# The S5 recurrence of a four-branch backbone: the blocked complex scan on VectorE and GpSimd becomes one scan instruction per row on turned inputs

## The chip, the cores and the metric

One core of a Trainium2 chip runs the whole program. The metric is the device time of one execution in microseconds. Three runs of the kernel before took 2464.4, 2462.11 and 3806.75 us, so the median is 2464.4 us.

The engines are named as in the profile: PE is TensorE (matmul) and PEld its weight load, DVE is VectorE, ACT is ScalarE, POOL is GpSimd, and SP is SyncE, whose queue issues nearly every DMA of this program.

## The reference, cut to what matters

There are two layers over 2048 latent tokens and 256 context tokens, with 1024 channels. Layer 0 is a Fourier mixer beside a neighbourhood attention. Layer 1 is a gated MLP (spatial gating within chunks of 128 tokens) beside a bidirectional S5, a bank of linear recurrences with complex states. The change is in S5 alone:

```python
def linear_scan(lam_bar, bu, h0, reverse):
    """h_t = lam_bar * h_{t-1} + bu_t along axis 1 (or reversed). bu: (B, L, G, P) complex; h0: (B, G, P) or None."""
...
def s5_direction(u_lat, u_ctx, ...):
    lam_bar, b_bar = s5_discretise(lam_re, lam_im, log_step, b_re, b_im)
...
    h_ctx = linear_scan(lam_bar, drive(u_ctx), None, reverse)
    h_end = h_ctx[:, 0] if reverse else h_ctx[:, -1]
    h_lat = linear_scan(lam_bar, drive(u_lat), h_end, reverse)
    return read(h_lat), (read(h_ctx) if with_ctx_out else None)
```

There are 32 groups of 16 channels, 64 complex states in each group and two directions. `drive` multiplies the inputs with B, `read` multiplies the states with C and keeps the real part. After it come GELU, a gated linear unit (GLU) and the output projection.

## The kernel before, in words

**Eight tokens at a time.** The kernel folds eight tokens into one step of the recurrence, so a sequence of 2304 tokens has 288 steps, and the factor between steps is the eighth power of a state's own factor. Three constant matrices per group are made once from the S5 weights by `s5_prep` and kept in DRAM: `min_d` (inputs of eight tokens to the drive of a step), `mo_d` (states to outputs) and `kp_d` (inputs to outputs inside a step). `s5_prep` runs early, at about 140 to 330 us, woven between the projections `v_proj(0)`, `v_proj(1)` and `v_proj(2)` of layer 0. Right after `v_proj(2)` comes `fourier_first`: 16 pieces, each with a load of a DFT table (`d`, L559), a load of `Z` (L561), two matmuls (L564), a copy to `a` (L566) and a write to `A_d` (L567), and then the context's part (L573, L577).

**The S5 stage.** `odd` calls `s5_quarter` four times (j = 0 to 3, eight groups each). In a quarter PE computes the drive (`pd`, L1634: 4 matmuls for each of 4 pairs of groups and 2 directions), ACT copies it to the tile `S` (L1636: 128 partitions x 2 directions x real/imaginary x 4 pairs x 288 steps), and then the recurrence runs in place on `S`, in three parts:

- The 288 steps are cut into 18 blocks of 16. Inside all blocks at once, 15 steps of complex multiply-add run over strided columns: per step five DVE instructions (L1655 to L1660), three of 128x288 and two of 128x144, whose columns lie 16 numbers apart.
- The blocks' last states are chained: 17 steps of five tiny DVE instructions on the same lines (128x16 and 128x8).
- The state before each block is multiplied into the block (L1697 to L1700), for direction 0 on DVE in instructions of 128x1020 and for direction 1 on POOL in instructions of 128x510.

The tables of the factor's powers are `pa`, from `pa_d` in DRAM. Then `O<-S` DMAs (L1710) bring real and imaginary parts of one group under each other, and for each of the quarter's 8 groups three matmuls make the output (`pg`, L1718 with `T`, L1719 and L1720 with `mo` and `O`), ACT applies GELU into `z` (L1722), DVE takes its maximum (L1723, `zmax`), and a DMA writes `z`.

**What runs beside it.** The eight `odd_pair` calls (256 tokens each) are the gated MLP: PE matmuls `pu` of 512 columns and, for the first four pairs, `pg` of 256 columns (`gd_pair`). Their DVE work is statistics (L1576), a chain of tiny instructions for a reciprocal root (`rs`, L122 to L136), and the gates (`Gs`, L1594 and L1598); two multiplications per 128 tokens are on POOL (L1588, L1607). Matmuls of a later pair wait for `Gs` of the pair before, because `Gs` frees their PSUM bank. After S5 come `glu`, which needs all of `z`, and `final`.

**What sets the order.** A scheduler places every instruction when the program is built, by its own estimate of time; at run time each engine and the SP queue work strictly in that order and wait at semaphores. An instruction that waits holds up everything behind it on its engine. Pools of SBUF that open after others have closed share their space, and a tile there waits until the old tiles under it are done with.

Of the kernel before, what the change touches and what calls it, by code (L numbers as in the profile page):

```python
# [9 lines left out]
F32 = mybir.dt.float32  # L10
# [4 lines left out]
OP = mybir.AluOpType  # L15
# [39 lines left out]
class Kern:  # L55
# [1060 lines left out]
    def s5_prep(self, between):  # L1116
# [7 lines left out]
        self.pa_d = self.dram.tile([128, 4, 2 * 2 * 2 * 4 * 17], F32, name="pa_d")  # L1124
        with self.pool_("s5p") as pool, ExitStack() as early:
# [46 lines left out]
            L8 = t([128, 2, 16, 32])  # L1172
            nc.vector.tensor_copy(L8[:, :, 0], PW[:, :, 8])
            for w in (1, 2, 4, 8):
                double(L8, 0, w)

            pa = t([128, 4, 2, 2, 2, 4, 17])
            L8r = t([128, 2, 16, 16])
            for i in range(16):
                nc.gpsimd.tensor_copy(L8r[:, :, i], L8[:, :, 15 - i, 16:32])  # L1180
            for part in range(2):
                for d in range(2):
                    src = L8[:, part, :, d * 16:(d + 1) * 16]
                    for rd in range(2):
                        nc.vector.tensor_copy(pa[:, :, part, d, rd, :, 16], src[:, 0].rearrange("p (j g) -> p j g", j=4))
                        v = src if d == 0 else L8r[:, part]
                        nc.vector.tensor_copy(pa[:, :, part, d, rd, :, 0:16], v.rearrange("p i (j g) -> p j g i", j=4))
            self.bq.dma_start(self.pa_d, pa.rearrange("p j a d r g i -> p j (a d r g i)"))
# [95 lines left out]
        with self.pool_("s5pk") as pool:  # L1284
# [11 lines left out]
            for q in range(8):  # L1296
# [18 lines left out]
                self.bq.dma_start(self.kp_d[q], kp)  # L1315

# [160 lines left out]
    def odd(self, mw):  # L1477
# [139 lines left out]
    def s5_quarter(self, pool, pb, j):  # L1617
        nc = self.nc
        pa = pool.tile([128, 2, 2, 2, 4, 17], F32, name=self.name("pa"), tag="pa", bufs=2)
        nc.sync.dma_start(pa, self.pa_d[:, j].rearrange("p (a d r g i) -> p a d r g i", a=2, d=2, r=2, g=4))  # L1620

        S = pb.tile([128, 2, 2, 4, 288], F32, name=self.name("S"), tag="S", bufs=2)
        for gp in range(4):
# [5 lines left out]
            for d in range(2):  # L1629
# [6 lines left out]
                nc.scalar.activation(S[:, d, :, gp, :], ps[:, :, 0:288], AF.Copy)  # L1636
        DS, RS = 8 * 288, 4 * 288
        t1 = pool.tile([128, 4 * 17 * 15], F32, name=self.name("t1"), tag="t1", bufs=1)
        t2 = pool.tile([128, 4 * 17 * 15], F32, name=self.name("t2"), tag="t2", bufs=1)

        def ap(off, dstep, n, step):
            return bass.AP(tensor=S.tensor, offset=S.offset + off, ap=[list(S.ap[0]), [dstep, 2], [288, 8], [step, n]])

        def half(off, dstep, n, step):
            return bass.AP(tensor=S.tensor, offset=S.offset + off, ap=[list(S.ap[0]), [dstep, 2], [288, 4], [step, n]])

        def tab(part):
            return pa[:, part]

        def step(cur, prev, ar, ai, n):  # L1650

            m = 16 * n
            x1 = t1[:, 0:m].rearrange("p (d q n) -> p d q n", d=2, q=8)
            x2 = t2[:, 0:m].rearrange("p (d q n) -> p d q n", d=2, q=8)
            nc.vector.tensor_tensor(x1, ap(*prev), ar, op=OP.mult)  # L1655
            nc.vector.tensor_tensor(x2, ap(*prev), ai, op=OP.mult)  # L1656
            nc.vector.tensor_tensor(ap(*cur), ap(*cur), x1, op=OP.add)  # L1657
            nc.vector.tensor_tensor(half(*cur), half(*cur), x2[:, :, 4:8], op=OP.subtract)  # L1658
            c2 = (cur[0] + RS,) + cur[1:]
            nc.vector.tensor_tensor(half(*c2), half(*c2), x2[:, :, 0:4], op=OP.add)  # L1660

        ar = [tab(p)[:, :, :, :, 16].rearrange("p d r g -> p d (r g)")[:, :, :, None].to_broadcast([128, 2, 8, 18])
              for p in range(2)]
        for i in range(1, 16):
            step((i, DS + 15 - 2 * i, 18, 16), (i - 1, DS + 17 - 2 * i, 18, 16), ar[0], ar[1], 18)
        a16 = [tab(p).rearrange("p d r g i -> p d (r g) i") for p in range(2)]

        def last(p):

            x = a16[p]  # L1670
            return bass.AP(tensor=x.tensor, offset=x.offset + 15, ap=[list(x.ap[0]), [8 * 17 - 15, 2], [17, 8], [1, 1]])

        ll = [last(0), last(1)]
        for k in range(1, 18):
            step((16 * k + 15, DS + (17 - k) * 16 - (16 * k + 15), 1, 1),
                 (16 * k - 1, DS + (18 - k) * 16 - (16 * k - 1), 1, 1), ll[0], ll[1], 1)
        for d in range(2):

            cur0 = d * DS + (16 if d == 0 else 1)
            car0 = d * DS + (15 if d == 0 else 16)  # L1680

            def v(off, q, i):
                return bass.AP(tensor=S.tensor, offset=S.offset + off,
                               ap=[list(S.ap[0]), [288, q], [16, 17], [1, 15] if i else [0, 15]])

            i0 = 0 if d == 0 else 1
# [184 lines left out]
```

## Time and profile before

| What | Value |
|---|---|
| median of the three runs | 2464.4 us |
| the profiled execution, its own time | 2459.69 us |
| its span, first to last instruction | 2457.9 us |
| PE busy | 2223.6 us (90%), 15860 matmuls |
| DVE busy | 1625.8 us (66%), 4343 instructions |
| POOL busy | 445.7 us (18%), 533 instructions |
| mean granted TensorE clock | 0.96 of full speed |

Busy time of PE includes matmuls that run at the lower clock, and their ends are modelled; so a stretch in which PE is busy throughout can still be one in which it does less than it could. What PE could do is read from the distance between the starts of consecutive matmuls where nothing holds it up. A row of the list by stretches gives busy time and count of each engine, the granted clock, the share of the DMA engines and GB/s.

### The profile page before, as it was taken

The page shows a single profiled execution, that of the slowest core. Times are in us where ns is not written, and L with a number is a line of the kernel's source. Part 1 is how long each engine was busy: PE and PEld are TensorE (multiplying, and loading weights), DVE is VectorE, ACT ScalarE, POOL GpSimd, SP SyncE. Part 2 cuts the span into 40 slices and gives each one's busy share as a digit, 9 for nine tenths or more (in the row PEclk, how much of TensorE's full clock was granted, in tenths as well). Part 3 has the DMA queues.
Part 4 walks back from the last instruction along what each step waited for, and adds up shares of the span by engine and source line. Part 5 has one row for each costly group of instructions (what it writes and reads, how often), then busy time and mean ns, then how long its engine had stood idle before and what let it go on. Part 6 is the DMA issues. An engine that isn't in the chain of part 4 may idle for free.

```text
span 2457.9 us, 43136 instructions
## 1 busy us (share of the span) xinstructions
PE 2223.6 (90%) x15860; PEld 1421.2 (58%) x15860; DVE 1625.8 (66%) x4343; ACT 1047.0 (43%) x2208; POOL 445.7 (18%) x533
## 2 busy tenths in 40 slices
PE   5999997998999999999878999978968787999998
PEld 2667784675766666666564566666534443544443
DVE  5888413466576666766686767751799998457555
ACT  4822232455556565555565555532211211244232
POOL 0123100122222222222340000000053154110000
PEclk8999998999999999999988999989989888999999
DMA  9845756224343343523433435552234532556332
GB/s 321 255 119 147 192 166 177 69 74 135 83 139 99 93 140 102 138 76 102 155 113 102 164 124 138 163 175 91 79 87 124 143 98 79 147 151 206 116 116 90
DMA packets 344165, 324.98 MB, mean 132 GB/s; under 512 B 93154, under 2 KB 290158, under 8 KB 343058
## 3 DMA queue, kind: packets, MB, share of 16 engines
q1 hardware_dynamic: 343842, 322.20, 44.1%
q8 instruction: 125, 2.05, 0.3%
q14 instruction: 86, 0.70, 0.1%
q10 hardware_dynamic: 112, 0.03, 0.0%
HBM read 210.10 MB, written 102.59 MB: 127 GB/s over the span
## 4 chain that ended last, share of the span: by engine, by line
PE 60%; DVE 22%; DMA 8%; issue 3%; ACT 3%; SPq 2%; POOL 1%; DVEq 0%; ACTq 0%; POOLq 0%
PE pg L181 36%; PE pu L181 6%; PE S L997 4%; PE PT L1016 4%; DVE S L1657 2%; PE pv L1030 2%; DVE t L1655 2%; DVE t L1656 2%; DVE S L1658 2%; DVE wl L190 1%; PE pa L331 1%; DMA wf<-in_w_in_even_dram 1%; DVE S L1660 1%; PE pv L1033 1%; DMA s_d<-s 1%
## 5 line engine op out<-in xcount | busy, mean ns | idle before, releaser
L181 PEld LDWEIGHTS <-wh 128*128 128x128 f16 x2944 | 280.0, 98 | 168.3 <-issue 10.8
L1000 DVE CUSTOM_DVE_ANT_0 P<-S,bias,slab 128x640 f32<-128x640 f32 (+2 forms) x216 | 193.6, 896 | 162.6 <-PE S L997 161.5
L189 ACT ACTIVATE ph<-PT 128x384 f16<-128x384 f32 (+1 forms) x408 | 172.6, 457 | 217.2 <-PE PT L1016 216.2
L181 PE MATMUL pu<-wh,h1p 128*128 128x512 f16 x768 | 191.2, 397 | 45.0 <-DVE Gs L1594 42.5
L181 PEld LDWEIGHTS <-h1p 128*128 128x128 f16 x1152 | 115.2, 101 | 192.4 <-issue 72.9
L949 POOL TENSOR_TENSOR bias<-G,masks 128x384 f32<-128x384 f32 (+1 forms) x144 | 152.6, 1060 | 349.6 <-DVE t L1000 326.9
L181 PEld LDWEIGHTS <-wl 128*128 128x128 f16 x1472 | 142.7, 100 | 116.2 <-issue 31.9
L190 DVE SCALAR_TENSOR_TENSOR pl<-PT,ph 128x384 f16<-128x384 f32 (+1 forms) x408 | 195.1, 508 | 13.9 <-ACT ph L189 12.5
L1002 ACT ACTIVATE P<-P,t 128x640 f32<-128x640 f32 (+2 forms) x216 | 181.2, 839 | 40.2 <-DVE t L1000 38.9
L181 PE MATMUL pg<-hh,wl 128*128 128x512 f16 (+1 forms) x800 | 183.6, 363 | 15.6 <-DVE stg L190 7.5
L181 PE MATMUL pg<-hl,wh 128*128 128x512 f16 (+1 forms) x800 | 181.9, 361 | 0.0
L181 PE MATMUL pg<-hh,wh 128*128 128x512 f16 (+1 forms) x800 | 180.6, 358 | 0.0
L181 PEld LDWEIGHTS <-yh 128*128 128x128 f16 x1088 | 106.5, 98 | 124.3 <-issue 0.8
L1016 PE MATMUL PT<-ident,P 128*128 128x128 f32 x1104 | 162.8, 277 | 11.5 <-DVE pl L190 9.6
L997 PEld LDWEIGHTS <-Q 128*128 128x128 f16 x1776 | 132.7, 99 | 62.7 <-issue 22.0
L997 PE MATMUL S<-K,Q 128*128 128x128 f16 (+1 forms) x1776 | 160.2, 234 | 1.8 <-DVE t L1000 1.7
L181 PE MATMUL pg<-wh,yl 128*128 128x512 f16 x544 | 133.1, 386 | 5.2 <-DVE yl L190 5.1
L1016 PEld LDWEIGHTS PT<-ident,P 128*128 128x128 f32 x1104 | 120.6, 142 | 20.7 <-issue 8.4
L1037 POOL TENSOR_TENSOR o<-o 128x64 f32<-128x64 f32 x216 | 73.3, 339 | 323.9 <-ACT o L1036 322.6
L181 PE MATMUL pg<-wh,yh 128*128 128x512 f16 x544 | 130.3, 379 | 0.0
L181 PE MATMUL pg<-wl,yh 128*128 128x512 f16 x544 | 130.2, 379 | 0.0
L156 DVE TENSOR_REDUCE t<-wf 128x1 f32<-128x1024 f32 x68 | 82.5, 1216 | 71.9 <-DMA wf<-in_w_in_odd_dram 25.4
(341 smaller groups left out, 4168.3 us busy)
## 6 DMA issues: line engine op xcount, KB each, us to landing
wada<-in_w_ada_dram SPq DMA_DIRECT2D x34, 512.0 KB
x<-in_x_dram SPq DMA_DIRECT2D x32, 512.0 KB
wf<-in_w_in_even_dram SPq DMA_DIRECT2D x28, 512.0 KB
V<-vs SPq DMA_DIRECT2D x192, 64.0 KB
K<-kd SPq DMA_DIRECT2D x96, 128.0 KB
wf<-in_w_in_odd_dram SPq DMA_DIRECT2D x20, 512.0 KB
Y<-ys SPq DMA_DIRECT2D x144, 64.0 KB
O<-S SPq DMA_DIRECT2D x64, 144.0 KB
```

Source lines behind the costliest of these rows:

```text
L156: nc.vector.tensor_reduce(m[:, i:i + 1], f, axis=AX.X, op=OP.max, apply_absolute_value=True)
L181: nc.tensor.matmul(ps, a(k), b(k), start=(n == 0), stop=(n == 3 * kb - 1))
L189: nc.scalar.activation(hi, src, AF.Copy, scale=scale)
L190: nc.vector.scalar_tensor_tensor(lo, src, scale, hi, op0=OP.mult, op1=OP.subtract)
L949: nc.gpsimd.tensor_tensor(q4(bv), gv, q4(masks[:, m0:m0 + 128 * nch]), op=OP.add)
L997: nc.tensor.matmul(S[:, at:at + m], u["q"], K[:, hl, off:off + m], start=(hl == 1), stop=(hl == 0))
L1000: nc.vector.tensor_tensor_reduce(P[:, 0:n], S[:, 0:n], u["B"][:, 0:n], u["negf"], 3.4e38, OP.add, OP.min, nm)
L1002: nc.scalar.activation(P[:, 0:n], P[:, 0:n], AF.Exp, bias=nm, scale=-1.0, accum_out=l)
L1016: self.nc.tensor.transpose(PT[:, c - a:c - a + 128], P[:, c:c + 128], self.ident)
L1030: nc.tensor.matmul(pv, ph[:, i * 128:(i + 1) * 128], vals[i][:, hd * 128:hd * 128 + 128], start=(i == 0), stop=False, skip_group_check=True)
L1037: nc.gpsimd.tensor_tensor(o["t"][:, hd * 64:(hd + 1) * 64], o2[:, 0:64], o2[:, 64:128], op=OP.add)
L1655: nc.vector.tensor_tensor(x1, ap(*prev), ar, op=OP.mult)
```

## The change

The factor of a step is split into its magnitude and its angle. The inputs of the recurrence are first turned back by the accumulated angle of their step, which leaves a recurrence with a real factor for real and imaginary part apart; after it the states are turned ahead by the same angles. The real recurrence is one DVE instruction per row of 288 steps (`tensor_tensor_scan`, L1674 of the changed kernel, in the order's rows a SCALAR_TENSOR_TENSOR that reads `mag`); for direction 1 it reads and writes the row backwards.

- `s5_quarter` is gone. `odd` goes through 8 halves (a half is 2 pairs of groups): `s5_states`, then `s5_out`. `S` is now one tile per direction and half, in 5 buffers.
- Per half and direction DVE has: `turned` over 288 steps (two multiplications of 128x1152, an addition and a subtraction of 128x576), 4 scans of 128x288, and `turned` over 256 steps (two of 128x1024, two of 128x512). POOL has no part in it.
- Per half and direction a DMA loads the angle table `E` (590 KB). `pa` is gone.
- `O` is fetched without the columns that aren't used: eight DMAs of 64 x 1 KB per pair of groups instead of four of 64 x 2 x 1152 B.
- `s5_prep` makes the angle tables: the powers of the turned unit by doubling, in tiles `turn` that live until `s5_prep` ends, and at its very end 8 tables of 128x2304 by a complex product, six DVE instructions of 128x1152 each, with a DMA of 1.2 MB to `rot_d` after each. The doublings and copies for `pa`, 16 of them on POOL, are gone.

```diff
@@ s5_prep, tables
-            L8 = t([128, 2, 16, 32])
...
-            for i in range(16):
-                nc.gpsimd.tensor_copy(L8r[:, :, i], L8[:, :, 15 - i, 16:32])
...
-            self.bq.dma_start(self.pa_d, pa.rearrange("p j a d r g i -> p j (a d r g i)"))
+            for w in (1, 2, 4, 8):
+                double(R, 1, w)
...
+            for T, n, o in ((R, 16, turn[0]), (RB, 18, turn[1])):
+                for r in range(2):
+                    nc.scalar.activation(o[:, r], T[:, r, 0:n].rearrange("p k q -> p q k"), AF.Copy)
@@ s5_prep, its end (pool s5pk)
+            tp = [t([128, 4, 18, 16]) for _ in range(2)]
+            for j in range(4):
+                for d in range(2):
+                    e = pool.tile([128, 2, 4, 288], F32, name=self.name("rot"), tag="rot", bufs=2)
...
+                    self.cmul(nc.vector, [e[:, r].rearrange("p g (b k) -> p g b k", k=16) for r in range(2)], x, y, tp)
+                    self.bq.dma_start(self.rot_d[j, d], e.rearrange("p r g n -> p (r g n)"))
@@ odd
-                for j in range(4):
-                    self.s5_quarter(self.s5a, s5b, j)
+                for i in range(8):
+                    self.s5_out(self.s5a, s5b, i // 2, i % 2, self.s5_states(self.s5a, s5b, i // 2, i % 2))
@@ s5_states (was the first part of s5_quarter)
+        S = [pb.tile([128, 2, 2, 288], F32, name=self.name("S"), tag="S", bufs=5) for _ in range(2)]
...
+            e = pb.tile([128, 2, 2, 288], F32, name=self.name("E"), tag="E", bufs=3)
+            nc.sync.dma_start(e, dap(self.rot_d, ...
...
         for d in range(2):
+            self.turned(pb, S[d], E[d], 0, 288, False)
             for ri in range(2):
+                for g in range(2):
+                    x = S[d][:, ri, g, :] if d == 0 else self.reversed(S[d][:, ri, g, :])
+                    q = 16 * d + 4 * j + 2 * h + g
+                    nc.vector.tensor_tensor_scan(x, self.mag8[:, q:q + 1].to_broadcast([128, 288]), x, 0.0, OP.mult, OP.add)
+            self.turned(pb, S[d], E[d], 31 - 30 * d, 256, True)
@@ turned (new)
+        nc.vector.tensor_tensor(t, swap, e[1], op=OP.mult)
+        nc.vector.tensor_tensor(x, x, e[0], op=OP.mult)
+        op = (OP.subtract, OP.add) if ahead else (OP.add, OP.subtract)
+        for r in range(2):
+            nc.vector.tensor_tensor(x[:, r], x[:, r], t[:, r], op=op[r])
@@ s5_out (was the last part of s5_quarter)
-            O = pb.tile([128, 2, 2, 288], F32, name=self.name("O"), tag="O", bufs=3)
+            O = pb.tile([128, 2, 2, 256], F32, name=self.name("O"), tag="O", bufs=3)
...
-                for ri in range(2):
-                    nc.sync.dma_start(O[64 * ri:64 * ri + 64, gpar], S[64 * gpar:64 * gpar + 64, :, ri, gp, :])
+                for d in range(2):
+                    for ri in range(2):
+                        nc.sync.dma_start(O[64 * ri:64 * ri + 64, gpar, d],
+                                          S[d][64 * gpar:64 * gpar + 64, ri, gp % 2, 31 - 30 * d:287 - 30 * d])
```

The order of DVE where one part of S5 meets the next, before (`rs` and `Gs` belong to an `odd_pair`, `S` and `t` to S5):

```order
L1700 TENSOR_TENSOR S_23782<-S_23782,t_5000_23852 128x4x17x15
L1697 TENSOR_TENSOR t_4999_23851<-S_23782,pa_23780 128x1020
L1577 BN_AGGR t_25756<-t_25810 128x2
L1698 TENSOR_TENSOR t_5000_23852<-S_23782,pa_23780 128x1020
L1699 TENSOR_TENSOR S_23782<-S_23782,t_4999_23851 128x4x17x15
L122 TENSOR_SCALAR rs_25814<-t_25756,slab_18826 128x2
L1594 SCALAR_TENSOR_TENSOR Gs_25878<-Gs_25878,pu_25853 128x512
L1700 TENSOR_TENSOR S_23782<-S_23782,t_5000_23852 128x4x17x15
L1655 TENSOR_TENSOR t_5058_24235<-S_24166,pa_24164 128x288
L124 TENSOR_SCALAR rs_25816<-rs_25814 128x2
L1656 TENSOR_TENSOR t_5059_24236<-S_24166,pa_24164 128x288
L126 TENSOR_SCALAR rs_25818<-rs_25816 128x2
```

The same place in the changed kernel (L1689 to L1693 are `turned`, L1674 is the scan, L1620 is `Gs`):

```order
L1693 TENSOR_TENSOR S_23645<-S_23645,t_23685 128x576 x2
L122 TENSOR_SCALAR rs_24782<-t_24724,slab_18932 128x2
L1674 SCALAR_TENSOR_TENSOR S_23645<-mag_1850,S_23645 128x288 x4
L124 TENSOR_SCALAR rs_24784<-rs_24782 128x2
L1689 TENSOR_TENSOR t_23694<-S_23645,E_23647 128x4x256
L1723 TENSOR_REDUCE zmax<-z_23596 128x1
L126 TENSOR_SCALAR rs_24786<-rs_24784 128x2
L1690 TENSOR_TENSOR S_23645<-S_23645,E_23647 128x4x256
L130 TENSOR_TENSOR rs_24788<-rs_24786 128x2
L1693 TENSOR_TENSOR S_23645<-S_23645,t_23694 128x2x256 x2
L132 TENSOR_TENSOR rs_24790<-rs_24788,rs_24782 128x2
L1620 SCALAR_TENSOR_TENSOR Gs_24846<-Gs_24846,pu_24821 128x512
```

The pair's chain still goes through between pieces of S5, one instruction at a time; the pieces are others. On PE the last output matmul of S5 now stands behind 433 `pu` matmuls counted from the first `pd`, where 908 stood before; the `odd_pair` work that was ahead of it comes after it.

The order of the SP queue at the end of `s5_prep`, before (`chan`, `dctx`, `d` and `Z` are loads of `fourier_first`, `vs` is what `v_proj` writes):

```order
L552 DMA chan<-in_k_chan_dram 128x256
L554 DMA dctx<-in_k_dctx_dram 128x1024
L545 DMA vs_128<-v_3436 128x256
L545 DMA vs_129<-v_3436 128x256
L559 DMA d_639_4426<-in_k_dft_dram 128x256
L561 DMA Z_4428<-fa_d 128x256
L559 DMA d_643_4436<-in_k_dft_dram 128x256
L561 DMA Z_4438<-fa_d 128x256
L545 DMA vs_128<-v_3466 128x256
```

And in the changed kernel:

```order
L545 DMA vs_130<-v_4485 128x256
L545 DMA vs_131<-v_4485 128x256
L1340 DMA rot_d<-rot_3934 128x2304
L545 DMA vs_130<-v_4515 128x256
L545 DMA vs_131<-v_4515 128x256
L1340 DMA rot_d<-rot_3942 128x2304
L552 DMA chan<-in_k_chan_dram 128x256
L554 DMA dctx<-in_k_dctx_dram 128x1024
L559 DMA d_655_4532<-in_k_dft_dram 128x256
L561 DMA Z_4534<-fa_d 128x256
```

Before, the first loads of `fourier_first` stood among the writes of `v_proj(1)`, long ahead of the end of `v_proj(2)`; now they stand behind the last write of `v_proj(2)` (`v_4515`) and behind the last angle table. Accordingly all 32 matmuls of L564 stand in PE's order behind the last matmul of `v_proj(2)`, where before 15 of them stood between its groups.

## Rows read from the trace of the kernel before

**Rows 1.** The page, busy time by engine: us, share of the span, count.

```profile
PE 2223.6 (90%) x15860; PEld 1421.2 (58%) x15860; DVE 1625.8 (66%) x4343; ACT 1047.0 (43%) x2208; POOL 445.7 (18%) x533
```

**Rows 2.** Stretches: us, PE, PEld, DVE, ACT, POOL busy (count), PEclk, DMA share, GB/s.

```profile
1695.00:1735.00 40.00, 36.10 (x219) 20.06 (x220) 11.10 (x26) 10.69 (x14) 0.00 (x0) 0.90 0.36 121
1735.00:1800.00 65.00, 63.84 (x377) 33.55 (x376) 62.55 (x184) 14.12 (x26) 9.22 (x6) 1.00 0.25 79
2110.00:2185.00 75.00, 73.39 (x372) 39.22 (x371) 38.49 (x96) 23.51 (x39) 11.58 (x8) 1.00 0.51 137
```

**Rows 3.** One stretch, only instructions on S: us, PE, DVE, ACT, POOL busy.

```profile
1735.00:2110.00 375.00, 0.00 (x0) 282.16 (x672) 15.67 (x25) 107.74 (x64) 0.90 0.38 106
```

**Rows 4.** Waits of PE, 1735 to 2110 us: us in total, times, longest.

```profile
PE pu L181 <- DVE Gs L1594: 42.5, 7, 11.1
```

**Rows 5.** PE in order of time: start us, us, operation [idle before]. First drive, last output.

```profile
1696.31 2.19 PE L1634 MATMUL pd<-U,mi 128*64 128x288 f32 x8
...
2125.57 0.59 PE L1720 MATMUL pg<-O,mo 128*128 128x256 f32 x2
```

**Rows 6.** PE in order of time, rates: distances of starts at full clock.

```profile
1846.29 0.59 PE L1720 MATMUL pg<-O,mo 128*128 128x256 f32 x2
1846.72 0.60 PE L181 MATMUL pg<-h1p,wl 128*128 128x256 f16 x4
1847.15 0.82 PE L181 MATMUL pg<-h1p,wh 128*128 128x256 f16 x6
1847.90 1.19 PE L1634 MATMUL pd<-U,mi 128*64 128x288 f32 x8
1849.02 0.66 PE L1612 MATMUL pT<-ident,sy 128*128 128x128 f32 x4
...
2130.53 3.62 PE L181 MATMUL pu<-wh,h1p 128*128 128x512 f16 x16
2133.99 1.89 PE L181 MATMUL pu<-wl,h1p 128*128 128x512 f16 x8
```

**Rows 7.** DVE in order of time: plain and held-up instructions of the S5 stage.

```profile
1821.98 1.50 DVE L1656 TENSOR_TENSOR t<-S,pa 128x288 f32<-128x288 f32 x1
1823.40 1.08 DVE L136 TENSOR_TENSOR rs<-rs,rs 128x2 f32<-128x2 f32 x1
...
1825.00 0.63 DVE L1657 TENSOR_TENSOR S<-S,t 128x288 f32<-128x288 f32 x1
1825.55 0.15 DVE L130 TENSOR_TENSOR rs<-rs 128x2 f32<-128x2 f32 x1
```

**Rows 8.** DVE in order of time: contiguous operands of 512 columns.

```profile
150.62 0.69 DVE L1112 TENSOR_TENSOR p<-p,p 128x512 f32<-128x512 f32 x1
```

**Rows 9.** DVE groups by shape, 1340 to 1640 us: busy us, mean ns; 1024 columns.

```profile
L1339 DVE TENSOR_TENSOR x<-x,y 128x1024 f32<-128x1024 f32 x18 | 22.0, 1223 | 0.3
L156 DVE TENSOR_REDUCE t<-wf 128x1 f32<-128x1024 f32 x14 | 17.1, 1220 | 23.0 <-DMA wf<-in_w_in_odd_dram 22.9
```

**Rows 10.** POOL groups, 1735 to 2110 us: busy us, mean ns.

```profile
L1588 POOL TENSOR_TENSOR vc<-vc,sgg 128x512 f32<-128x512 f32 x12 | 16.6, 1403 | 494.9 <-ACT vc L1587 494.9
```

**Rows 11.** Stretches at the end of the preparation; columns as in rows 2.

```profile
282.00:328.00 46.00, 46.00 (x535) 40.56 (x533) 10.00 (x43) 15.81 (x43) 0.00 (x0) 1.00 0.70 180
328.00:361.00 33.00, 33.00 (x275) 29.09 (x273) 4.25 (x10) 8.06 (x18) 0.00 (x0) 1.00 0.49 153
361.00:377.00 16.00, 10.98 (x36) 8.07 (x35) 0.43 (x1) 5.40 (x10) 0.00 (x0) 0.79 0.67 221
```

**Rows 12.** PE in order of time: pieces of the Fourier step and what follows.

```profile
328.08 1.46 PE L564 MATMUL pg<-Z,d 128*128 128x256 f32 x6
...
360.76 2.32 PE L564 MATMUL pg<-Z,d 128*128 128x256 f32 x10
...
376.47 1.88 PE L573 MATMUL pg<-dctx,zc 128*128 128x512 f32 x4
```

**Rows 13.** One line's instructions: ns min/median/max, first and last start in us.

```profile
L1700 DVE TENSOR_TENSOR S<-S,t x8: 1208/1688/2085, 1802.4 to 2072.7; 128x1020 f32<-128x1020 f32 x8
```

More of the change, by code (lines that the diff above doesn't have):

```diff
@@ L1188, in s5_prep @@
-            self.bq.dma_start(self.pa_d, pa.rearrange("p j a d r g i -> p j (a d r g i)"))
+            sq = [t([128, 32]), t([128, 32])]
+            nc.vector.tensor_tensor(sq[0], mag, mag, op=OP.mult)
+            nc.vector.tensor_tensor(sq[1], sq[0], sq[0], op=OP.mult)
+            nc.vector.tensor_tensor(self.mag8, sq[1], sq[1], op=OP.mult)
+            R, RB = t([128, 2, 17, 32]), t([128, 2, 18, 32])
+            un = [t([128, 2, 32]) for _ in range(3)]
+            nc.vector.tensor_copy(un[0][:, 0], co)
@@ new lines, in s5_prep @@
+            nc.vector.tensor_copy(un[0][:, 1, 0:16], si[:, 0:16])
+            nc.vector.tensor_scalar(un[0][:, 1, 16:32], si[:, 16:32], -1.0, None, op0=OP.mult)
+            for k in range(3):
+                x = [un[k][:, r] for r in range(2)]
+                o = [un[k + 1][:, r] for r in range(2)] if k < 2 else [R[:, r, 1] for r in range(2)]
+                self.cmul(nc.vector, o, x, x, [z[:, 0] for z in tp])
+            for T in (R, RB):
+                nc.gpsimd.memset(T[:, 0, 0], 1.0)
+                nc.gpsimd.memset(T[:, 1, 0], 0.0)
@@ L1644, in half @@
[L1644 to L1671, printed above, removed]
@@ new lines, in reversed, with turned @@
+    def reversed(self, a):
+        n = a.shape[-1]
+        return bass.AP(tensor=a.tensor, offset=a.offset + n - 1, ap=[list(a.ap[0]), [-1, n]])
+    def turned(self, pb, S, E, at, n, ahead):
+        nc = self.nc
+        t = pb.tile([128, 2, 2, 288], F32, name=self.name("t"), tag="t", bufs=1)[:, :, :, 0:n]
+        x = S[:, :, :, at:at + n]
+        swap = bass.AP(tensor=x.tensor, offset=x.offset + 576, ap=[list(x.ap[0]), [-576, 2]] + [list(v) for v in x.ap[2:]])
+        e = [E[:, r, None, :, at:at + n].to_broadcast([128, 2, 2, n]) for r in range(2)]
+        nc.vector.tensor_tensor(t, swap, e[1], op=OP.mult)
[3 more added lines that the diff above has]
+            nc.vector.tensor_tensor(x[:, r], x[:, r], t[:, r], op=op[r])
@@ new lines, in s5_out @@
+    def s5_out(self, pool, pb, j, h, S):
+        nc = self.nc
+        if h == 0:
+            self.T = T = pool.tile([128, 8, 128], F32, name=self.name("T"), tag="T", bufs=1)
+            for s in range(8):
+                nc.sync.dma_start(T[16 * s:16 * s + 16], dap(self.kp_d, 8 * j * 32 * 240 + (7 - s) * 16,
+                                                            [[240, 16], [32 * 240, 8], [1, 128]]))
+        T = self.T
+        for gp in (2 * h, 2 * h + 1):
+            O = pb.tile([128, 2, 2, 256], F32, name=self.name("O"), tag="O", bufs=3)
```

78 lines of the change are left out of this document (25 added, 53 removed).

## The prediction

> **What bounds the kernel now.** By the page PE is the fullest engine and POOL the emptiest [rows 1], so the first question is whether the S5 stage is an exception. The list by stretches says that it is. From 1735 us on DVE is full, and at first PE is too, at the full clock [rows 2]. Then PE stops keeping up. Asked for the instructions on the tile S alone, the stretch 1735 to 2110 us shows 282.16 us of DVE and 107.74 us of POOL in 375 us, at a granted clock of 0.90 [rows 3]. PE's largest wait there is for `Gs`, 42.5 us in 7 pieces [rows 4]: `Gs` is the odd pairs' own work, which stands in DVE's queue between pieces of S5. POOL's part makes this worse: while it runs, a 128x2 instruction of the root chain takes 1.08 us and a 128x288 one 1.50 us, where 0.15 and 0.63 us are seen right after it has ended [rows 7].
>
> What PE loses is the distance between the work that it has and the time that it takes. At full clock a 512-column f16 matmul takes (2133.99 - 2130.53) / 16 = 0.216 us, a 256-column one 0.43 / 4 = 0.108, an f32 one of 256 columns 0.43 (each f32 matmul shows as two in a row's count), a drive matmul 1.12 / 4 = 0.28 [rows 6]. The program's order has, from the first drive to the last output of S5, 908 of the first kind (196 us), 384 (41), 96 (41) and 128 (36), and 96 small ones that I put at 0.16 us on the mean from L1612's row (15, so 329 in all). The trace shows 1696.31 to 2126.2, which is 430 us [rows 5]. So 101 us are lost. Of these some 8 belong to the start (PE is busy for 36.1 of the first 40 us, at 0.90 of the clock [rows 2]), which the change leaves alone. **At most about 91 us are to be had in this stage.**
>
> **The change, part by part.** The sum is made against the profiled execution, 2459.7 us; the median is 4.7 us above it.
>
> *DVE in the S5 stage.* Removed: what rows 3 show, 282 us on DVE and 108 on POOL. Added, per half and direction: two multiplications of 1152 columns, two of 576, two of 1024 and two of 512, all on contiguous operands. Plain contiguous instructions take 0.69 and 1.22 us for 512 and 1024 columns [rows 8, 9], that is 1.04 ns for a further column, so 0.76 us for 576 and 1.36 us for 1152. One half and direction takes 2 x (1.36 + 0.76 + 1.22 + 0.69) = 8.06 us, and 16 of them 129 us. Neighbours overlap by some 0.08 us, so I count 118. Then 64 scans of 288 columns, which no row shows. Low end: the contiguous rate, 0.69 - 224 x 1.04 ns = 0.46 us (29 us in all). High end: the slowest 288-column row, 1.50 us (96 us). I take the strided row of the same size, 0.63 us [rows 7], because a recurrence that needs its own last result is more likely below than at the full rate: 40 us. [...]
>
> Beside S5, DVE's order holds to the last piece about 36 us of the three or four odd pairs and of 27 maxima (50 instructions of 256 or 512 columns at 0.4 to 0.7 us, about 50 tiny ones at 0.15). POOL keeps two multiplications per 128 tokens at 1.40 us [rows 10]; in four pairs that is 16 x 1.4 = 22 us in which DVE runs at about half its rate, so 11 us more. DVE: 118 + 40 + 36 + 11 = 205 us, and it begins some 12 us after the first drive. PE's order holds to the last output 433 x 0.216 + 41 + 41 + 36 + 8 = 220 us. The two end together, at about 217 to 220 us. So PE becomes the bound, but narrowly, and each in-order queue still waits for the other at every half: S goes from PE by ACT to DVE, by the SP queue into `O`, and back to PE. I leave 15 us of the 91 as lost, between 0 (DVE always ahead) and 45 (half stays). The 110 us of `pu` matmuls that now come behind S5 run as the pairs at 2110 to 2185 us do, where PE is busy for 73.39 of 75 us [rows 2]: 3 us.
>
> *E, O and the SP queue.* 16 loads of 590 KB are new, 9.4 MB, and `O` takes 128 DMAs for 64. The DMA engines are at 0.38 in this stretch [rows 3]; the same traffic in 235 instead of 390 us gives 0.63, and E at the page's rates for such stages adds about 0.15. That fits. I cost it at nothing beyond the 15 us, since E is loaded a half ahead; if that cover is gone, the start of each half is late, and PE waits at L1719.
>
> *The preparation.* Powers by doubling for powers by doubling, POOL's 16 copies gone: near zero, and at best a gain of 4 us. New at its end: 8 x 6 multiplications of 1152 columns, 48 x 1.27 = 61 us of DVE, beside `v_proj(2)`. DVE is busy for 10 of 46 and 4.25 of 33 us there [rows 11], so it rises to about 75 of 79 us: it just fits. But `fourier_first` doesn't fit any more. Before, five groups of three L564 matmuls, 1.5 pieces each, ran between the projections at about 1.3 us a group (6.5 us of PE), and the other 8.5 pieces after 360.76 took 376.47 - 360.76 = 15.7 us, 1.85 each [rows 12], because loads and writes of three buffers pace them: PE is busy for 11 of 16 us and DMA at 0.67 [rows 11]. Now their loads stand on the SP queue behind the last angle table, and all 16 pieces come after the projections: 16 x 1.85 = 29.6 us in place of 15.7 + 6.5. That is 7.4 us more, plus about 3 us for the first load's landing and 2 us where 9.4 MB of table writes meet a DMA share of 0.70 [rows 11]. I take 12 us. Low end -4 (DVE ends early, loads keep ahead), high end +30 (the multiplications push the evictions of `v_proj(2)` as well).
>
> *Sum.* -91 + 15 + 3 + 12 = -61: 2398.7 us against the profiled execution, **2403 us** as a median.
>
> **The rivals.**
>
> 1. *The chain through DVE stays the bound.* If a scan takes 1.5 us, DVE's sum rises by 56 us to 261, some 50 us behind PE, and about half of the 91 us stays lost: 2440 to 2450 us. The same comes of an SP queue whose `O` fetches wait for S and hold up the loads behind them. For it: DVE and PE end within a few us of each other in my sum. Against: even then DVE has less than before. Chance 0.22.
> 2. *The preparation costs its high end.* 30 us in place of 12: about 2421 us. For it: DVE near full beside the evictions for 75 us, and a large write after each table. Chance 0.10.
> 3. *Slower than before.* A scan's step waits for the result of the step before it, and the latency isn't hidden. Before, S5's last DVE piece came 2072.7 - 1696.31 = 376 us after the first drive [rows 5, 13]; now DVE is at 12 + 165 us without scans, so the gain is used up, with 12 us of preparation, at 64 scans of 2.9 us, 10 ns for each step. At 5 us a scan DVE takes 320 us longer than without scans, and the time is about 2460 + 130 = 2590 us. For it: nothing in the trace is a true recurrence. Against: a reduction, which also carries a running value, takes 1.22 us for 1024 columns in rows 9, the rate of a plain addition. Chance 0.06.
> 4. *It doesn't free what it means to.* PE's wait at `Gs` is the pair's chain itself, 16 dependent instructions, and other waits move up: 2450 to 2465 us. Against: the chain is 16 x 0.15 us once POOL is quiet. Chance 0.04.
>
> **How the numbers follow.** The forecast has 0.58; its own range, from no stall and cheap preparation (2375) to the middle of both upper ends (2427), is met below 2415 in about nine of eleven cases. 2415 us is 2% below the median, and 2% is about what a measurement of this kernel can tell from no change. Faster by over 2%: 0.48 from the forecast, 0.04 from rival 2, 0.05 from rival 1 in its mild form, 0.57. Slower by over 2%: rival 3 and a little of unknown stalls, 0.07. Within 2%: 0.36. The range reaches from 2370 us to 2450 us, which takes in the upper end of rival 1 and leaves out rival 3, most of rival 4 and a gain beyond the 91 us.
>
> **What would show it.** Right: in the stretch of S5 the granted clock back near 1.00, PE's waits for `Gs` a few us in all, the last L1720 about 235 to 240 us after the first drive, scan rows (L1674) near 0.6 us, and L573 10 to 15 us later than 376 us. Wrong: DVE still at 95% and PE waiting at L1719 or for `Gs` (rival 1), waits of PE for `v` between 280 and 360 us (rival 2), scan rows of several us (rival 3). A forecast like this fails most easily where two engines come out within 5 us of each other on paper.

## The result, and the profile after

The changed kernel takes 2424.4 us (median of 4 runs, 2421.3 to 2431.3) where the kernel before took 2463.3 (median of 4), about 39 us less. By the fast runs alone, which leave out one of 3806.8 us of the kernel before, the ratio is 0.985, with a 95% interval of 0.982 to 0.988: faster, by less than 2%. The profiled execution took 2425.1 us with a span of 2423.3.

Three points on PE's own time line split the difference: L573, the first matmul behind the Fourier pieces, where the preparation ends; the first drive of S5; and the end of the span.

| | before | after | difference |
|---|---|---|---|
| start to L573 | 376.5 | 403.0 | +26.5 |
| L573 to the first drive | 1319.8 | 1320.6 | +0.8 |
| first drive to the end | 761.6 | 699.7 | -61.9 |

So the S5 stage gave 62 us, and the preparation took 27 of them back. The page's first line, where POOL stood at 445.7 us [rows 1]:

```profile
PE 2219.7 (92%) x15860; PEld 1421.6 (59%) x15860; DVE 1579.7 (65%) x3949; ACT 1050.9 (43%) x2212; POOL 336.3 (14%) x457
```

**The S5 stage.** The first drive and the last output of the changed kernel on PE, in order of time; they answer to [rows 5]:

```profile
1723.65 2.19 PE L1665 MATMUL pd<-U,mi 128*64 128x288 f32 x8
...
1980.29 0.59 PE L1720 MATMUL pg<-O,mo 128*128 128x256 f32 x2
```

That is 257 us, where it was 430. A row by stretch has us, PE, PEld, DVE, ACT and POOL busy with counts, the granted clock, the DMA share and GB/s. The whole stage in the kernel before:

```profile
1696.30:2126.20 429.90, 362.47 (x1886) 199.80 (x1886) 360.51 (x891) 83.78 (x161) 140.26 (x88) 0.91 0.38 107
```

Five pieces of this stage in the changed kernel:

```profile
1723.00:1763.00 40.00, 37.31 (x219) 20.64 (x220) 31.15 (x44) 10.55 (x14) 0.00 (x0) 0.85 0.60 191
1763.00:1828.00 65.00, 60.12 (x344) 36.56 (x342) 64.65 (x97) 17.73 (x35) 6.52 (x4) 0.97 0.65 179
1828.00:1880.00 52.00, 46.72 (x226) 23.67 (x224) 33.23 (x61) 8.64 (x16) 2.49 (x2) 1.00 0.71 200
1880.00:1930.00 50.00, 46.10 (x281) 27.31 (x281) 47.34 (x62) 13.43 (x27) 2.82 (x2) 1.00 0.76 213
1930.00:1981.00 51.00, 48.13 (x278) 33.02 (x276) 38.11 (x64) 12.75 (x27) 6.61 (x4) 0.97 0.57 156
```

DVE is no longer full throughout: 214 of 258 us. Two rows for the whole stage of the changed kernel, all engines first, then the instructions on S alone (us, PE, DVE, ACT, clock, DMA, GB/s):

```profile
1723.60:1980.70 257.10, 237.48 (x1338) 140.64 (x1338) 214.48 (x324) 62.79 (x118) 18.44 (x12) 0.96 0.66 187
...
1723.60:1980.70 257.10, 0.00 (x0) 176.89 (x192) 20.82 (x32) 0.96 0.66 187
```

S costs DVE 177 us and GpSimd nothing, where it was 282 and 108 [rows 3]. PE's waits in the same stretch (us in total, times, longest); no row names `Gs`, which took 42.5 us before [rows 4]:

```profile
PE pg L1720 <- DMA O<-S: 3.6, 2, 1.9
PE pg L1718 <- DMA O<-S: 3.1, 1, 3.1
PE pg L1719 <- DMA O<-S: 2.7, 1, 2.7
PE pd L1665 <- ACT S L1667: 2.7, 1, 2.7
...
PE pd L1665 <- DMA O<-S: 1.4, 1, 1.4
```

Rather more than half of what PE waits for now is `O`, the copy of the states: 10.8 of the 20 us in which it is idle. On DVE, in order of time, a product, four scans, and a pair of L1693 alone and beside GpSimd:

```profile
1739.28 1.36 DVE L1690 TENSOR_TENSOR S<-S,E 128x1152 f32<-128x1152 f32 x1
...
1765.49 2.69 DVE L1674 TENSOR_TENSOR_SCAN S<-mag,S 128x288 f32<-128x288 f32 x4
...
1771.01 1.29 DVE L1693 TENSOR_TENSOR S<-S,t 128x512 f32<-128x512 f32 x2
...
1795.49 3.32 DVE L1693 TENSOR_TENSOR S<-S,t 128x512 f32<-128x512 f32 x2
```

Four scans in a row take 2.69 us, 0.67 each. The last row shows the same pair of instructions at 3.32 instead of 1.29 us: GpSimd's multiplications of the odd pairs are still there (two of L1614, 3.10 us from 1795.16).

**The preparation.** PE, DVE and the waits of PE at its end, in the changed kernel. PE in order of time (in brackets the idle time before, and its releaser):

```profile
356.68 1.04 PE L181 MATMUL pg<-wh,hh 128*128 128x256 f16 x8
373.98 6.63 PE L564 MATMUL pg<-Z,d 128*128 128x256 f32 x16 [16.27 <-DMA Z<-fa_d]
...
402.09 1.10 PE L564 MATMUL pg<-Z,d 128*128 128x256 f32 x4 [0.22 <-DMA Z<-fa_d]
403.02 1.45 PE L573 MATMUL pg<-dctx,zc 128*128 128x512 f32 x3
```

DVE, the last eviction of `v_proj(2)` and the last product of the last angle table:

```profile
360.57 0.42 DVE L190 SCALAR_TENSOR_TENSOR v<-pg,v 128x256 f16<-128x256 f32 x1
...
364.95 1.36 DVE L1114 TENSOR_TENSOR rot<-p,p 128x1152 f32<-128x1152 f32 x1
```

And the SP queue right behind it:

```profile
366.33 0.32 SPq L1340 DMA_DIRECT2D rot_d<-rot  x1
366.75 0.38 SPq L552 DMA_DIRECT2D chan<-in_k_chan_dram  x1
367.18 0.91 SPq L554 DMA_DIRECT2D dctx<-in_k_dctx_dram  x1
368.14 1.20 SPq L559 DMA_DIRECT2D d<-in_k_dft_dram  x1
369.38 0.50 SPq L561 DMA_DIRECT2D Z<-fa_d  x1
```

PE has nothing for 16.27 us: the table is finished at 366.3, the first `Z` is issued at 369.4 and is there at 374.0. Then the 16 pieces take 29.0 us, 1.81 each.

### The profile page after: what moved, and what is told of

Read it like the earlier page. It is cut to its first block, busy times and chain, and to the rows that moved or that the text cites. A ratio compares the mean times of both kernels' runs of the same rounds, so it can differ in the third digit from the quotient of the medians.

```text
span 2423.3 us, 42852 instructions
## 1 busy us (share of the span) xinstructions
PE 2219.7 (92%) x15860; PEld 1421.6 (59%) x15860; DVE 1579.7 (65%) x3949; ACT 1050.9 (43%) x2212; POOL 336.3 (14%) x457
## 5 line engine op out<-in xcount | busy, mean ns | idle before, releaser
L181 PE MATMUL pu<-wh,h1p 128*128 128x512 f16 x768 | 179.9, 379 | 1.6 <-DMA h1p<-h 1.6
L181 PEld LDWEIGHTS <-hh 128*128 128x128 f16 x1152 | 115.5, 100 | 15.7
```

Of the source, the lines that this page charges most:

```text
L181: nc.tensor.matmul(ps, a(k), b(k), start=(n == 0), stop=(n == 3 * kb - 1))
```

## The experiments

Two times are read from each trace: when L573 starts (the preparation), and the time from the first drive to the end of the span (S5 and all that follows). The second is better than the stage alone, since an edit also moves `pu` matmuls over the stage's end. Six kernels with the changed kernel's preparation have L573 between 403.0 and 408.6 us; five with its S5 have 698.2 to 700.5 us from the first drive to the end. Differences below 6 us in the first and 2.5 us in the second are not read. The whole times of the kernels that were run once are 2425.4 us (one table), 2428.0 (two writes), 2418.6 (a third of the products), 2447.3 (scans twice), 2423.4 (no recurrence), 2436.4 (with GpSimd), 2422.3 (O in 64) and 2429.5 (z from ScalarE); they carry the scatter of all the stages that the edit leaves alone, so the two times above are read instead.

**Loads apart** (`p1_loads_apart`).

```diff
-                    with self.pool_("fft") as fp, self.stream("f"):
+                    with self.pool_("fft", side="right") as fp, self.stream("f"):
...
-            for j in range(4):
+            for j in range(8):
                 for d in range(2):
-                    e = pool.tile([128, 2, 4, 288], F32, name=self.name("rot"), tag="rot", bufs=2)
+                    e = pool.tile([128, 2, 2, 288], F32, name=self.name("rot"), tag="rot", bufs=2)
```

(The smaller tables lie in `rot_d` in another order, and the loads of `E` follow it.)

> The changed kernel with the angle tables made two state groups at a time (buffers half as large) and the pool of fourier_first put on the other side of SBUF, so that its loads share no space with the tables. The 61 us of table multiplications on DVE stay. Theory (the loads' wait): the 26.5 us that the preparation lost are PE's wait for Z until the last table is out of its buffer, and the pieces that then stand alone; L573 comes at 360 to 372 us in place of 403, and the whole takes 2385 to 2397 us. Rival (DVE time): the multiplications hold up the evictions of v_proj(2); L573 stays later than 390 us, and the whole takes 2410 to 2425 us.

Measured: 2407.8 us (median of 4), ratio to the kernel before 0.976 (0.972 to 0.979), against 0.985 for the change. L573 came at 383.75. One stretch of this kernel (columns as above), and PE in order of time:

```profile
328.00:361.00 33.00, 33.00 (x324) 29.09 (x322) 26.81 (x52) 11.03 (x27) 0.00 (x0) 1.00 0.93 287
```

```profile
370.59 1.89 PE L564 MATMUL pg<-Z,d 128*128 128x256 f32 x8
...
383.75 2.97 PE L573 MATMUL pg<-dctx,zc 128*128 128x512 f32 x4
```

DVE still makes all the tables (26.8 of 33 us here, and the last product ends at 387 us, behind L573), yet PE is never idle in that stretch. So 19 of the 26.5 us were the loads' wait for the last table, and not DVE's time. The run changes the side of the pool and the size of the tables together, and no run has the smaller tables alone; but the first load of `Z` is issued at 302 us here, 85 us before the last product ends, which smaller tables in the loads' way could not give. L573 missed its 360 to 372, and the time its range; the DMA engines are at 0.93 in the stretch, and PE still waits 6.3 us for `Z` in all, but whether one comes of the other no run shows. Of the 19 us only 11.7 arrive at the first drive in the profiled run; from L573 to there it takes 1328 us, and 1326 to 1327 in the two kernels at the end of this section, against 1318 to 1326 in the others. What takes these few us is open.

**Two writes** (`p3_two_writes`) and **a third of the products** (`p2_third_of_products`).

```diff
-                    self.bq.dma_start(self.rot_d[j, d], e.rearrange("p r g n -> p (r g n)"))
+                    if j == 0:
+                        self.bq.dma_start(self.rot_d[0, d], e.rearrange("p r g n -> p (r g n)"))
```

> The changed kernel with all 48 table multiplications, but only two of the eight tables written (and read for all groups, so the states come out of wrong angles): 7.1 of 9.4 MB of writes are left out. In the measured runs with the changed kernel's preparation L573 came at 403 to 409 us. Theory (the tables' last multiplications hold the space that the loads of fourier_first wait for): L573 still at 393 to 405 us. Rival (the table writes fill the transfer engines): 375 to 387 us.

```diff
-                    self.cmul(nc.vector, [e[:, r].rearrange("p g (b k) -> p g b k", k=16) for r in range(2)], x, y, tp)
+                    for r in range(2):
+                        nc.vector.tensor_tensor(e[:, r].rearrange("p g (b k) -> p g b k", k=16), x[r], y[r], op=OP.mult)
```

> The changed kernel with 16 of the 48 table multiplications (two products to a table in place of the complex product, so wrong angles) and all eight writes, each behind its own products: some 41 us of DVE left out. Theory (the last multiplications): the loads stand among the last groups of v_proj(2) again, L573 at 380 to 393 us. Rival (the writes of 9.4 MB): 395 to 409 us.

Measured: with two of the eight writes L573 at 402.5, with a third of the products at 394.3. In the kernel with two writes, the stretch in which DMA has little left to do, PE's wait, and a wait of the SP queue at L552, the load of `chan`, first of the loads of `fourier_first`:

```profile
328.00:361.00 33.00, 29.14 (x278) 25.36 (x275) 31.35 (x40) 5.68 (x16) 0.00 (x0) 1.00 0.17 48
```

```profile
PE pg L564 <- DMA Z<-fa_d: 22.7, 9, 14.1
```

```profile
SPq L552 <- DVE rot L1114: 4.5, 1, 4.5
```

The DMA share falls to 0.17 and nothing is won: the writes did not cost the 26.5 us. And the last table write stands 55 us ahead of the loads here, yet the first of them waits 4.5 us for DVE's last product (L1114 to `rot`): the loads wait for the tables' space itself, not only for their turn on the queue. With a third of the products the loads do stand among the groups of `v_proj(2)` again, but only 9 us come back, and L573 lies 1 us above its range of 380 to 393: the eight writes follow each other faster there, and PE waits 8.4 us for `bs` behind them.

**One table** (`a1_one_table`).

```diff
+            e = pool.tile([128, 2, 4, 288], F32, name=self.name("rot"), tag="rot", bufs=2)
...
+            self.cmul(nc.vector, [e[:, r].rearrange("p g (b k) -> p g b k", k=16) for r in range(2)], x, y, tp)
             for j in range(4):
                 for d in range(2):
-                    e = pool.tile([128, 2, 4, 288], F32, name=self.name("rot"), tag="rot", bufs=2)
...
                     self.bq.dma_start(self.rot_d[j, d], e.rearrange("p r g n -> p (r g n)"))
```

> The changed kernel with one angle table worked out instead of eight, written to all eight places: 42 of 48 multiplications of 1152 columns are left out (the states of the other groups come out of wrong angles), all writes stay. Theory (the loads' wait): with the tables early, the loads of fourier_first are early too, L573 at 365 to 378 us, the whole 2390 to 2402 us, about as with the loads apart. Rival (DVE time): as here 365 to 378 us, but then loads apart with all multiplications must come out at least 15 us later than this one. Rival (the table writes, 9.4 MB, cost): L573 stays later than 390 us.

Measured: 2425.4 us, L573 at 402.9, as with all tables; of the three readings only the last, that the writes cost, has that number. PE's largest wait from 250 to 410 us in this kernel, and the stretch with the writes:

```profile
PE pg L1319 <- DMA bs<-bst_d: 17.4, 4, 8.1
```

```profile
282.00:328.00 46.00, 34.60 (x376) 30.21 (x374) 14.70 (x36) 10.13 (x28) 0.00 (x0) 0.90 0.95 304
```

With one table the eight writes of 1.18 MB come within 22 us, the loads of `bs` (64 KB each) queue behind them, and PE stops in the middle of the projections instead of at their end. So this run did not price the products; it shows that the writes are cheap only while products space them out, as the run with two writes could not show.

**Every scan twice** (`a4_scan_twice`) and **no recurrence** (`a3_no_recurrence`).

```diff
                     nc.vector.tensor_tensor_scan(x, self.mag8[:, q:q + 1].to_broadcast([128, 288]), x, 0.0, OP.mult, OP.add)
+                    nc.vector.tensor_tensor_scan(x, self.mag8[:, q:q + 1].to_broadcast([128, 288]), x, 0.0, OP.mult, OP.add)
```

> The changed kernel with every scan issued twice (the states come out wrong): 64 more scans, 64 x 0.70 = 45 us more on DVE in the S5 stage, which has 214 us of work in 257. Theory (DVE has slack, the queue of loads and PE set the stage): the stage from the first drive to the last output grows by 5 to 20 us. Rival (DVE's chain sets the stage): it grows by 35 to 45 us, to 292 to 302.

```diff
-                    nc.vector.tensor_tensor_scan(x, self.mag8[:, q:q + 1].to_broadcast([128, 288]), x, 0.0, OP.mult, OP.add)
+                    nc.vector.tensor_tensor(x, self.mag8[:, q:q + 1].to_broadcast([128, 288]), x, op=OP.mult)
```

> The changed kernel with each scan replaced by a plain multiplication of the same rows by the same factor (no recurrence, so the states are wrong). Theory (half rate): the plain one takes 0.40 to 0.48 us where the scan takes 0.70, DVE has 64 x 0.26 = 17 us less, and the stage stays within 6 us of 257, since DVE has slack. Rival (DVE's chain sets the stage): the stage falls by 12 to 20 us.

Measured: with scans twice the stage takes 287.4 us, 30 more, between the two ranges; from the first drive to the end it is 719.5 us, 20 more than 699.7; the stage grew by more than that since 52 matmuls came into it from behind. Without the recurrence the stage takes 251.2, just within the 6 us of its theory, and from the first drive to the end it is 694.6, 5 less. DVE's work on S in the two kernels (us, PE, DVE, ACT, clock, DMA, GB/s), and four plain instructions in a row in the second:

```profile
1726.00:2013.60 287.60, 0.00 (x0) 222.47 (x256) 20.78 (x32) 0.93 0.60 169
```

```profile
1727.10:1978.50 251.40, 0.00 (x0) 158.24 (x192) 20.79 (x32) 0.97 0.67 192
...
1744.51 1.55 DVE L1674 TENSOR_TENSOR S<-mag,S 128x288 f32<-128x288 f32 x4
```

Adding 45.6 us to DVE's 176.9 costs 20 us, so some 25 us of them found room; taking 18.7 away gives 5. DVE has slack, and what it does still counts in part: neither reading holds alone. The recurrence costs (2.69 - 1.55) / 4 = 0.29 us in 288 steps, 1.0 ns a step, about as much again as the 1.04 ns of a further column of a plain instruction [rows 8, 9]; so by the column the scan goes at about half the rate of a plain instruction, as its theory had it. By itself the plain instruction has a median of 0.45 us, the scan of 0.73.

**The kernel before without GpSimd in S5** (`b3_before_dve_only`) and **the change with GpSimd** (`a5_ahead_on_pool`).

```diff
-            eng, m = (nc.vector, 4) if d == 0 else (nc.gpsimd, 2)
-            if d == 0:
-                x1, x2 = t1, t2
...
+            eng, m = nc.vector, 4
+            x1, x2 = t1, t2
```

> The kernel before with one part of the change alone: the fix-up of direction 1 on DVE, as direction 0's, instead of on GpSimd. DVE gets 32 instructions of 1020 columns more, 32 x 1.2 = 39 us, and no longer runs beside 108 us of GpSimd. Theory (the steps' sum on DVE was the bound; GpSimd gave about what it took): from the first drive to the last output 415 to 445 us where it was 430, the whole within 15 us of the kernel before. Rival (the sharing with GpSimd was the main loss, and the scan would not have been needed): 370 to 405 us, the whole 25 to 60 us faster.

```diff
-            self.turned(pb, S[d], E[d], 31 - 30 * d, 256, True)
+            self.turned(pb, S[d], E[d], 31 - 30 * d, 256, True, nc.gpsimd if d else nc.vector)
```

> The changed kernel with GpSimd back: the turning ahead of direction 1 (8 x 4 instructions, 2 of 1024 and 2 of 512 columns) runs on GpSimd. DVE has 8 x 3.8 = 30 us less. Theory (the two engines share, and DVE loses more than it gives away): GpSimd takes 60 to 90 us for it, DVE's instructions beside it 1.5 to 2.5 times their time, DVE's busy time in the stage doesn't fall below 210 us, and the stage is 5 to 30 us longer than 257. Rival (a second engine helps): DVE's sum falls by some 25 us and the stage to 245 to 257 us.

Measured: the kernel before without GpSimd's part takes 2445.8 us (one run; the kernel before beside it 2461.7), and from its first drive to the end 746.3 us in place of 761.6. The first answers to its theory, 423 us for the stage, though the whole fell by 15.9 us where it had within 15. S on DVE there (us, PE, DVE, ACT, clock, DMA, GB/s), and with GpSimd in the changed kernel (with POOL behind ACT), then all engines in the latter:

```profile
1697.70:2120.60 422.90, 0.00 (x0) 297.85 (x704) 20.81 (x32) 0.96 0.40 112
```

```profile
1724.90:1997.70 272.80, 0.00 (x0) 160.65 (x160) 20.84 (x32) 69.78 (x32) 0.95 0.62 177
...
1724.90:1997.70 272.80, 247.65 (x1361) 144.39 (x1361) 213.28 (x293) 62.93 (x118) 85.80 (x44) 0.95 0.62 177
```

108 us of GpSimd became only 298 - 282 = 16 us on DVE, though 32 instructions of 1020 columns, some 39 us, were added: more than half of what GpSimd took off, it had cost DVE in longer instructions. The other way round, in the changed kernel, GpSimd takes 70 us for 30 us of DVE's work; DVE's work on S falls by 16, but all that DVE does in the stage only from 214 to 213, the stage is 16 us longer, as its theory had it, and from the first drive to the end it takes 709.7 us, 10 more. A product of 1152 columns, 1.36 us when alone, takes 3.40 beside it (the second row is GpSimd's, in the same kernel):

```profile
1818.52 3.40 DVE L1691 TENSOR_TENSOR S<-S,E 128x1152 f32<-128x1152 f32 x1
```

```profile
1817.35 3.35 POOL L1691 TENSOR_TENSOR S<-S,E 128x1024 f32<-128x1024 f32 x1
```

So in the kernel before leaving GpSimd out gives 15 of the 62 us by itself. The other 47 are the rest of the change together: the scan on turned inputs, the halves and the narrower `O`; no run takes these apart. In the two rows just above DVE's instruction, 1.36 us when alone, ends 1.22 us after GpSimd's, at 1821.92 and 1820.70 us.

**O in 64 transfers** (`s1_o_in_64`) and **z from ScalarE's queue** (`s2_z_from_act`).

```diff
-        S = [pb.tile([128, 2, 2, 288], F32, name=self.name("S"), tag="S", bufs=5) for _ in range(2)]
+        SS = pb.tile([128, 2, 2, 2, 288], F32, name=self.name("S"), tag="S", bufs=SB)
+        S = [SS[:, d] for d in range(2)]
...
-                for d in range(2):
-                    for ri in range(2):
-                        nc.sync.dma_start(O[64 * ri:64 * ri + 64, gpar, d],
...
+                for ri in range(2):
...
+                    nc.sync.dma_start(O[64 * ri:64 * ri + 64, gpar], x)
```

(`SB` is 3, and `x` the rows of both directions.)

> The changed kernel with the states of both directions in one tile and O fetched in 64 transfers of both directions instead of 128: 64 issues of 0.56 us, 36 us, less on the SP queue. Theory (the SP queue is behind PE's waits for O): PE's waits for O, 10.9 us in the stage now, fall below 4 us, and the stage from the first drive to the last output takes 240 to 250 us instead of 257. Rival (S is late from DVE, or the two directions in one tile cost a wait of their own): 254 to 265 us.

```diff
-                nc.sync.dma_start(dap(self.z_d, (j * 128 + 16 * g) * 2048, [[256, 8], [2048, 16], [1, 256]]), z)
+                nc.scalar.dma_start(dap(self.z_d, (j * 128 + 16 * g) * 2048, [[256, 8], [2048, 16], [1, 256]]), z)
```

> The changed kernel with the 32 writes of z issued from ScalarE's queue, right behind the activation that makes z, instead of from SP's: 32 x 0.63 = 20 us less on the SP queue, up to as much more on ScalarE, which is busy for about a quarter of the stage. Theory (the SP queue is behind the waits for O): the stage takes 245 to 253 us instead of 257. Rival (S is late from DVE): 254 to 262 us.

Measured: with 64 transfers the stage takes 239.5 us, with 60 matmuls fewer in it, and 688.7 from the first drive to the end, 11 less. With z from ScalarE 262.9, just above both of its ranges, and 696.1, 4 less from the first drive on, with 48 more matmuls in the stage. PE's waits for `O` in the first of the two:

```profile
PE pg L1721 <- DMA O<-S: 3.6, 3, 2.4
...
PE pg L1720 <- DMA O<-S: 1.5, 1, 1.5
```

They fall from 10.8 to 5.1 us, a little over what was expected; DVE's work on S was the same within 2 us, so the 11 us don't come from DVE's work. But the first run changes two things. It issues 64 transfers fewer, some 40 us of the SP queue where 72 went before, and it gives `S` room for three halves where five one-direction tiles hold two and a half. That room counted too, at least on ACT, which in the changed kernel waits before it writes a new `S` until `O` has been copied out of an old one:

```profile
ACT S L1667 <- DMA O<-S: 10.9, 2, 10.2
```

With 64 transfers no such wait is left; with z from ScalarE, where the queue has 32 issues less and `S` no more room, it is 12.0 us, and 4 us came back. So the fetches of `O`, by their issues or by how long they hold `S`, were behind about 11 us of what PE still lost; how much each had is open.

**Both together** (`c1_both`, `c2_both_fewer_loads`). The first joins loads apart and O in 64; the second adds this and z from ScalarE:

```diff
-                mo = pool.tile([128, 2, 144], F32, name=self.name("mo"), tag="mo", bufs=3)
-                nc.sync.dma_start(mo, dap(self.mo_d, (8 * j + g) * 256 * 144, [[144, 128], [128 * 144, 2], [1, 144]]))
+            mo2 = pool.tile([128, 2, 2, 144], F32, name=self.name("mo"), tag="mo", bufs=2)
+            nc.sync.dma_start(mo2, dap(self.mo_d, (8 * j + 2 * gp) * 256 * 144, [[144, 128], [128 * 144, 4], [1, 144]]))
```

> Loads apart and O in 64 transfers together, nothing left out. If the two gains add (16.6 us from the one, and 11 us from the first drive to the end of the program from the other): 2393 to 2401 us, ratio to the kernel before 0.970 to 0.975. If they overlap: 2402 to 2410 us.

> As the kernel with both, and the SP queue relieved further: mo fetched for two groups in one transfer (16 instead of 32 issues of 0.42 us) and the writes of z issued from ScalarE's queue (32 issues of 0.63 us less on SP). Theory (the SP queue still sets part of the S5 stage): 3 to 10 us below the kernel with both. Rival (that queue has enough room once O takes 64): within 3 us of it.

Measured (medians of 4): 2395.1 us, ratio to the kernel before 0.972 (0.970 to 0.975), and 2402.0 us, 0.974 (0.973 to 0.976). The gains add, and the first is the fastest kernel of the study, 29 us below the change. Relieving the queue further gives nothing more: the second is 7 us above the first, which neither of its readings had. In the first the stage is down to (columns as above):

```profile
1709.30:1951.00 241.70, 227.86 (x1278) 133.98 (x1278) 211.43 (x323) 61.27 (x115) 18.69 (x12) 0.97 0.68 196
```

DVE has 211 of 242 us there and PE 228: what is left in the stage are these two.

## Why the prediction was right or wrong

The direction and the bound of the kernel before were right, and 2424 lies in the range, but the point, 2403, was 21 us low. Its likeliest outcome, faster by over 2% (0.57), did not come; the measured 1.5% is the case of 0.36. In profiled executions, 2398.7 us forecast and 2425.1 measured, the miss is 26.4 us: by the terms of the sum the S5 stage gave 11 us less than forecast, the preparation cost 14.5 more, and 0.8 lie between. Of its own signs two came, `Gs` gone and scans near 0.6 us; the clock (0.96), the stage (257 us for 235 to 240) and L573 (26.5 us later for 10 to 15) fell short. Two slips in its sums matter little: 101 less 8 is 93 and not 91, and no stall with the cheapest preparation makes 2372 and not 2375.

- **DVE bounds S5 through `Gs`, and 101 us are lost there: right.** `Gs` left PE's list, and the stage became 62 us shorter for the same work; the granted clock rose from 0.91 over the stage to 0.96.
- **The part beside GpSimd: right, and now with a price.** Leaving GpSimd out alone gave 15 us where the change gave 62.
- **The scan at 0.63 us, between 0.46 and 1.50: nearly right.** 0.67 undisturbed and 0.70 on the mean of 64, 45 us where 40 were counted. That a recurrence runs below the plain rate was the author's guess, and the run without it shows it: 0.67 us a scan for 0.39 a plain instruction. Rival 3 needed 2.9 us.
- **DVE's sum of 205 us: 214 measured.** Scans were 45 us for 40. The turning took 132, where 118 were counted and up to 11 more for GpSimd; everything else took 38 for 36.
- **PE as the bound with 15 us of stalls: the size was off.** PE is busy for 237 us and idle for 20. The work at full clock was 220, so 17 us went elsewhere: the first 40 us ran at 0.85 of the clock and lost 6, two later stretches at 0.97 lost 3.5, and the remaining 7 or so are not accounted for by any row (changes between kinds of matmul are a guess). With 20 us idle that makes 37 lost, where the sum had left 10 and 15. The prediction took all that PE lost before, bar the start, as waiting that could go. But of those 101 us PE was idle for 67, and for 33 it was busy longer than its work at full clock; after the change these are 20 and 17.
- **E and O at nothing: wrong by up to the 11 us that 64 transfers won.** It named the cover, E loaded a half ahead, and that held: no wait of PE or DVE for E shows. But it weighed bytes and not issues: 128 issues of `O` at 0.56 us are 72 us of a queue that has 257, and `O` is what PE and ACT waited for. Rival 1 had named fetches of `O` that hold up the queue as its second cause; the runs come close to that, in a mild form.
- **110 us of `pu` matmuls behind S5 at 3 us extra: right.** From the last output to the end it takes 110.6 us more than before.
- **The preparation at 12 us: wrong, and the failed step is the landing of the first load.** 16 pieces at 1.85 us were counted as 29.6 us, and 29.0 were measured. But about 3 us, which no row shows, were given for the first load, and PE idled for 16.3. The sum compared 75 us of DVE work with 79 of room and let the last table end with `v_proj(2)`; it ended 9 us after PE's last group, then came three other loads, then 4.6 us of landing. And the projections ended 3 us earlier without the interleaved pieces, not 6.5.
- **Rival 2 gave the right size, 2421 us, for the wrong reason.** It held DVE's load on the evictions or the writes responsible. PE's waits for `v` are 8.1 us over the preparation, 8.6 before; the writes can go without effect; and with the loads apart 19 us come back with every product in place. The order of the SP queue, shown ahead of the prediction, had the cause in it: the loads behind the last table.

## What to carry to other kernels

When work is added at the end of a stage, ask first whose buffers stand in the space that the next stage loads into: here 61 us of DVE work beside the projections cost 19 us because the next loads took its space, and moving a pool to the other side of SBUF, with smaller tables, gave them back at that place and 17 us of the whole time. When a stage shrinks, count the issues of its DMA queue against the new length, and how long a fetch holds its buffer, not only the bytes. And of what an engine loses, count as waiting only the time in which it is idle: here 67 of 101 us.

## What the runs showed of the hardware

A scan of 288 steps in f32 takes 0.67 us in a row of four, 0.29 us more than a plain product of the same row. Eight writes of 1.18 MB issued within 22 us held up loads of 64 KB behind them on the queue and cost PE 17.4 us of waiting, while the same writes spaced by about 9 us cost nothing that shows: with two of the eight, L573 came at 402.5 us for 403.0. And 64 instructions of GpSimd that took 108 us saved DVE only 16 us of its work on `S`.
